# Two transformer blocks on one core: the U products of the expert layer as 512 columns, and one-hot rows by a compare with a pointer

## The chip, the cores and the metric

One Trainium2 chip, one NeuronCore. The metric is the device time of one launch in microseconds (us), as the median over runs.

## The reference

Two blocks run one after the other on 256 tokens of width 1024, all in f32. The first block (attention and a gated feed-forward layer) and the attention and convolution of the second take the first half of the time and are not touched. The change lies in the last layer, a product-key expert layer with 16384 experts. Cut to what matters:

```python
q = (xc @ peer_wq).reshape(TOKEN_CHUNK, PEER_HEADS, PEER_DQ)
v1, i1 = lax.top_k(s1, 16); v2, i2 = lax.top_k(s2, 16)      # s1, s2: scores against 128 keys each
top_s, pos = lax.top_k(v1[..., :, None] + v2[..., None, :], 16)
e = i1 * 128 + i2 at pos;  g = softmax(top_s)                # 8 heads x 16 experts for each token
h = gelu(einsum('cd,chkd->chk', xc, peer_u[e]))
y = einsum('chk,chkd->cd', g * h, peer_v[e])
```

## The kernel before, in words

The kernel does not gather expert rows. It multiplies all 16384 rows of U with all 256 tokens, in 128 blocks of 128 experts, takes the gelu, multiplies it with a gate that is zero for every expert that a token did not choose, and multiplies the result with all rows of V.

**Precision.** TensorE multiplies in fp32r. Each f32 operand is split into a high part (a copy that rounds, on ScalarE) and a low part (the difference, on GpSimd for U, on VectorE for V), and three products are summed: high by high, high weight by low x, low weight by high x.

**U products** (`u_products`, lines 1034 to 1048). For each pair of blocks one PSUM bank `ph` of 512 columns holds two halves of 256 tokens. For each block there are 16 matmuls of 256 columns with the high weights (lines 1042 and 1043: each of the 8 weight chunks is loaded twice, once for `xTh` and once for `xTl`) and 8 with the low weights (line 1046). `u_finish` (line 1050) is called one pair later: it applies the gelu on ScalarE and, for tokens whose gates are there already, multiplies by the gate on VectorE (line 1057).

**Choice of experts** (`choose`, line 909). VectorE finds the top 16 and the indices for each half of the tokens; at the end TensorE transposes the result (`psel`, line 964) and VectorE copies it to `selT` (line 965). The main loop (line 1075) deals out 4000 ns of these steps by fixed estimates to each pair of U blocks, which places 30 blocks ahead of the end of the choice.

**Gates** (`gates`, line 977). For each token a one-hot row of the first key index, times the gate weight in a high and a low part, is multiplied with a one-hot row of the second index: one matmul `pw` of 256 columns (line 1003) gives that token's 128 by 128 gates in two parts. The one-hot rows are made by `choices` (line 985) for four tokens at once: line 990 compares an iota with both indices (1024 elements per partition), line 992 multiplies the first half of that with the two gate parts (1024 elements). ScalarE then copies parts of `pw` out (lines 1009 and 1011), VectorE adds or multiplies them into the tables `GA` and `GB` (lines 1013, 1016, 1019). The function `between` (line 1088) deals the 128 token pairs out over the U blocks that are left but four, in quarters of a block pair.

**V products** (line 1102) come last: 512 columns each, three for each weight part, with the gated activations as stationary operand. They need the gates of all tokens.

**What sets the order.** The program is written in one order; a scheduler turns that into one queue for each engine when the kernel is built, and on the chip each queue runs in order, with waits on semaphores. PSUM has 8 banks: four under tag `a` (the bank of `gate`, and those of `ph`), four under tag `b` (`scratch` with the iota, and `pw`). The raw weights come in by DMA from the SP queue (line 1028), four blocks deep, with three buffers each for the split parts.

Of the kernel before, what the change touches and what calls it, by code (L numbers as in the profile page):

```python
# [10 lines left out]
F32 = mybir.dt.float32  # L11
F32R = mybir.dt.float32r
U32 = mybir.dt.uint32
AF = mybir.ActivationFunctionType
ALU = mybir.AluOpType
# [3 lines left out]
P = 128  # L19
T = 256  # L20
D = 1024
KC = D // P
# [32 lines left out]
def block_pair_kernel(ctx: ExitStack, tc: tile.TileContext, x, gains, convw, norm_final, w_in, w_up_a, w_up_b,  # L55
                      w_out, w_gate, w_up, w_down, w_in_2, qg, kg, w_out_2, wq, keys, u_t, v_tab, final_g,
                      rope1, rope2, masks, out, dbg=None):
    nc = tc.nc
    mm = nc.tensor.matmul
# [6 lines left out]
    def bank(tag, name):  # L66
        return ps.tile([P, 512], F32, tag=tag, name=name)
# [83 lines left out]
    with ExitStack() as dense:  # L151
# [8 lines left out]
        low = {"every": 2}  # L160
# [72 lines left out]
        def xt_pair(pool, tag, kc=KC):  # L233
            return (pool.tile([P, kc, T], F32R, tag=tag + "h", name=tag + "h"),
                    pool.tile([P, kc, T], F32R, tag=tag + "l", name=tag + "l"))
# [287 lines left out]
        with ExitStack() as b2:  # L523
# [15 lines left out]
            for c0 in range(0, DFF, 512):  # L539
# [28 lines left out]
                for i, w_ in enumerate((cwh.bitcast(F32), cwl)):  # L568
                    sh = [P, j1 - j0, P]
# [20 lines left out]
            for b in range(2):  # L590
                drain(gemm_tok(fT, w_down, NFF, 512 * b, 512, add_to_x(b), "fd"))
                feat_split(hT, X, gnf, "n3", range(4 * b, 4 * b + 4))
                sl = slice(512 * b, 512 * b + 512)
# [250 lines left out]
            nc.sync.dma_start(dbg["x3"], X)  # L844

        peer = ctx.enter_context(tc.tile_pool(name="peer", bufs=1, side="right", reuse_waits="tile"))
        xT = xt_pair(peer, "xT")
        selT = peer.tile([P, 3, T], F32, tag="selT", name="selT")
        up = ctx.enter_context(tc.tile_pool(name="up", bufs=2, side="right", reuse_waits="tile"))
        tkx = ExitStack()  # L850
# [4 lines left out]
        iota = scratch[:, 0:P]  # L855
# [114 lines left out]
    def parts(lo, hi):  # L970

        for t_, base, n in ((GA, 0, BLK_A), (GB, BLK_A, NBLK - BLK_A)):
            a, b = max(lo, base), min(hi, base + n)
            if a < b:
                yield t_[:, a - base:b - base], a, b

    def gates(tk2):

        gate = bank("a", "gate").rearrange("p (a t) -> p a t", a=2)
        gh = up.tile([P, 2, T], F32R, tag="gh", name="gsh")[:, 0]  # L980
        nc.scalar.copy(gh, selT[:, 2])
        nc.vector.tensor_copy(gate[:, 0], gh.bitcast(F32))
        nc.vector.tensor_sub(gate[:, 1], selT[:, 2], gh.bitcast(F32))

        def choices(t4):

            sh = [P, 2, 4, P]
            eq = tk2.tile(sh, F32R, tag="eq", name=f"eq_{t4}")
            o1 = tk2.tile(sh, F32R, tag="o1", name=f"o1_{t4}")
            nc.vector.tensor_tensor(eq, iota.unsqueeze(1).unsqueeze(1).to_broadcast(sh),  # L990
                                    selT[:, 0:2, t4:t4 + 4].unsqueeze(3).to_broadcast(sh), op=ALU.is_equal)
            nc.vector.tensor_tensor(o1, eq[:, 0].bitcast(F32).unsqueeze(1).to_broadcast(sh),  # L992
                                    gate[:, :, t4:t4 + 4].unsqueeze(3).to_broadcast(sh), op=ALU.mult)
            return eq, o1

        now = choices(0)
        for t4 in range(0, T, 4):
            ahead = None
            for i in range(2):
                t0 = t4 + 2 * i  # L1000
                pw = bank("b", f"pw{t0}").rearrange("p (j a n) -> p j a n", j=2, a=2)
                for j in range(2):
                    mm(pw[:, j], lhsT=now[0][:, 1, 2 * i + j], rhs=now[1][:, :, 2 * i + j], start=True, stop=True)  # L1003
                if i == 0 and t4 + 4 < T:
                    ahead = choices(t4 + 4)
                x_ = done["blocks"]
                if x_:
                    w_ = up.tile([P, 2, P], F32, tag="gll", name=f"w_{t0}")
                    nc.scalar.copy(w_[:, :, :x_], pw[:, :, 1, :x_])
                for g, a, b in parts(x_, NBLK):  # L1010
                    nc.scalar.copy(g[:, :, t0:t0 + 2].rearrange("p b t -> p t b"), pw[:, :, 1, a:b])
                if x_:
                    nc.vector.tensor_tensor(pw[:, :, 0, :x_], pw[:, :, 0, :x_], w_[:, :, :x_], op=ALU.add)
                for g, a, b in parts(0, x_):
                    g = g[:, :, t0:t0 + 2].rearrange("p b t -> p t b")
                    nc.vector.tensor_tensor(g, pw[:, :, 0, a:b], g, op=ALU.mult)
                for g, a, b in parts(x_, NBLK):
                    g = g[:, :, t0:t0 + 2].rearrange("p b t -> p t b")
                    nc.vector.tensor_tensor(g, pw[:, :, 0, a:b], g, op=ALU.add)
                done["tokens"] = t0 + 2  # L1020
                if i == 0:
                    yield 1
            now = ahead
            yield 1

    def load_block(src, i, name, eng):
        raw = up.tile([P, D], F32, tag="raw", name=f"{name}raw{i}", bufs=4)
        nc.sync.dma_start(raw, src)
        hi = up.tile([P, D], F32R, tag="hi", name=f"{name}hi{i}", bufs=3)
        lo = up.tile([P, D], F32R, tag="lo", name=f"{name}lo{i}", bufs=3)  # L1030
        split(hi, lo, raw, eng)
        return hi, lo

    def u_products(b, between=lambda part: None):
        ph = bank("a", f"ph{b}")
        xh, xl = xT
        for i in range(2):
            hi, lo = load_block(u_t[b + i].rearrange("p k e -> p (k e)"), b + i, "u", nc.gpsimd)
            o = ph[:, i * T:(i + 1) * T]
            for k in range(KC):  # L1040
                sl = slice(k * P, (k + 1) * P)
                mm(o, lhsT=hi[:, sl], rhs=xh[:, k], start=k + i == 0, stop=False)  # L1042
                mm(o, lhsT=hi[:, sl], rhs=xl[:, k], start=False, stop=False)  # L1043
            between(2 * i)
            for k in range(KC):
                mm(o, lhsT=lo[:, k * P:(k + 1) * P], rhs=xh[:, k], start=False, stop=k + i == KC)  # L1046
            between(2 * i + 1)
        return b, ph.rearrange("p (b t) -> p b t", b=2)

    def u_finish(b, ph):  # L1050
        n = done["tokens"]
# [22 lines left out]
    b = 0  # L1074
    while spend(steps, 4000) and b < BLK_A:
        now = u_products(b)
        if pending:
            u_finish(*pending)
        pending = now
        b += 2  # L1080
# [3 lines left out]
    GB = gwb.tile([P, NBLK - BLK_A, T], F32, tag="GB", name="GB")  # L1084
    with tc.tile_pool(name="tk2", bufs=2, side="right", reuse_waits="tile") as tk2:
        steps = gates(tk2)
        first, rounds = b, (NBLK - b) // 2 - 2
        def between(part):
            quarter = 4 * ((b - first) // 2) + part + 1
            drain(steps, max(0, -(-(T // 2) * quarter // (4 * rounds)) - done["tokens"] // 2))  # L1090

        while b < NBLK:
            now = u_products(b, between)
            if pending:
                u_finish(*pending)
            pending = now
            b += 2
# [124 lines left out]
```

## Time and profile before

| | us |
|---|---|
| median of 3 runs | 1328.95 |
| lowest and highest run | 1327.55, 1329.12 |
| the profiled execution, its own time | 1327.62 |
| its span, first to last instruction | 1325.8 |
| mean granted TensorE clock | 0.988 |
| PE, VectorE (DVE), ScalarE (ACT), GpSimd (POOL) busy | 97%, 70%, 53%, 50% |

PE is the matmul engine and PEld its weight loads. Matmuls overlap in a pipeline, and so do VectorE instructions to a smaller degree: the duration of one is longer than the time from its start to the start of the next. Where the cost of many in a row is wanted, the distance between starts is the one to read.

### The profile page before, as it was taken

The numbers are of one execution on the slowest core, as the hardware profiler recorded it, in microseconds if no ns is written. First come the engines' busy times: TensorE is split into PE (matmuls) and PEld (weight loads), VectorE is DVE, ScalarE is ACT, GpSimd is POOL, SyncE is SP. The second block draws the span as 40 slices with busy tenths as digits, with TensorE's granted clock in tenths as the row PEclk, the third lists the DMA queues.
The fourth block names the chain that finished last, engine by engine and source line by source line (L and its number), as shares of the span: only waits on it lengthen the run. The fifth ranks groups of instructions, "written<-read, shape, count | busy, mean of one in ns | idle before, by whom it ended". The sixth has DMA issues, their size and how long they took to land.

```text
span 1325.8 us, 22837 instructions
## 1 busy us (share of the span) xinstructions
PE 1286.9 (97%) x8585; PEld 1179.9 (89%) x8585; DVE 925.2 (70%) x1984; ACT 704.6 (53%) x1263; POOL 669.4 (50%) x322
## 2 busy tenths in 40 slices
PE   7799999999999979999999999999999999999997
PEld 7689989999889859999999999999988888888885
DVE  6775546766327964799599999999955555555555
ACT  5256655444456736454566666656544444444443
POOL 5565485777468728567877777777700000000001
PEclk9899999999999979999999999999999999999999
DMA  8343344654754415245655555555566666666663
GB/s 294 132 159 128 128 159 159 193 189 130 237 173 144 144 64 193 79 131 172 180 169 162 165 169 161 165 169 161 161 197 197 192 191 195 194 195 193 191 192 109
DMA packets 85646, 222.65 MB, mean 168 GB/s; under 512 B 6304, under 2 KB 15904, under 8 KB 85536
## 3 DMA queue, kind: packets, MB, share of 16 engines
q1 hardware_dynamic: 84960, 220.12, 52.9%
q8 instruction: 67, 1.10, 0.3%
q10 hardware_dynamic: 576, 1.08, 0.2%
q14 instruction: 43, 0.35, 0.1%
HBM read 220.13 MB, written 1.05 MB: 167 GB/s over the span
## 4 chain that ended last, share of the span: by engine, by line
PE 89%; DVE 7%; ACT 2%; DMA 1%; issue 0%; POOL 0%; SPq 0%; ACTq 0%; DVEq 0%
PE po L1107 26%; PE ph L1042 8%; PE ph L1043 8%; PE ph L1046 8%; PE pw L1003 2%; PE fu L221 2%; PE fu L220 2%; PE fg L222 2%; PE fu L222 2%; PE fg L221 2%; PE fg L220 2%; PE fd L197 2%; PE fd L199 2%; PE fd L198 2%; PE g L220 1%; PE wq L221 1%
## 5 line engine op out<-in xcount | busy, mean ns | idle before, releaser
L121 POOL TENSOR_TENSOR wlo<-raw,whi 128x1024 fp32r<-128x1024 f32 (+3 forms) x134 | 301.1, 2254 | 184.9 <-ACT whi L120 171.7
L121 POOL TENSOR_TENSOR ulo<-uraw,uhi 128x1024 fp32r<-128x1024 f32 x128 | 309.2, 2418 | 110.6 <-PE ph L1046 47.5
L120 ACT CAST whi<-raw 128x1024 fp32r<-128x1024 f32 (+3 forms) x174 | 167.9, 970 | 192.5 <-PE fd L198 30.5
L121 DVE TENSOR_TENSOR vlo<-vraw,vhi 128x1024 fp32r<-128x1024 f32 x128 | 157.1, 1227 | 153.2 <-ACT vhi L120 153.2
L1042 PE MATMUL ph<-xTh,uhi 128*128 128x256 f32 x1024 | 252.9, 284 | 0.0
L1043 PE MATMUL ph<-xTl,uhi 128*128 128x256 f32 x1024 | 252.5, 284 | 0.0
L120 ACT CAST vhi<-vraw 128x1024 fp32r<-128x1024 f32 x128 | 135.0, 1055 | 180.2 <-PE po L1107 175.4
L120 ACT CAST uhi<-uraw 128x1024 fp32r<-128x1024 f32 x128 | 134.5, 1052 | 157.1 <-issue 109.0
L1042 PEld LDWEIGHTS ph<-xTh,uhi 128*128 128x128 f32 x1024 | 197.6, 193 | 0.2 <-DVE GB L1057 0.2
L1043 PEld LDWEIGHTS ph<-xTl,uhi 128*128 128x128 f32 x1024 | 197.4, 193 | 0.0
L1143 POOL TENSOR_TENSOR X<-X,fg 128x512 f32<-128x512 f32 x4 | 5.1, 1279 | 351.5 <-ACT GA L1140 351.5
L1046 PE MATMUL ph<-xTh,ulo 128*128 128x256 f32 x1024 | 144.0, 283 | 0.0
L1107 PE MATMUL po<-vhi,gh 128*128 128x512 f32 x512 | 138.3, 389 | 0.0
L1107 PE MATMUL po<-vhi,gll 128*128 128x512 f32 x512 | 138.3, 389 | 0.0
L1107 PE MATMUL po<-vlo,gh 128*128 128x512 f32 x512 | 138.3, 389 | 0.0
L1046 PEld LDWEIGHTS ph<-xTh,ulo 128*128 128x128 f32 x1024 | 132.2, 192 | 0.0
L1107 PEld LDWEIGHTS po<-vlo,gh 128*128 128x128 f32 x512 | 96.1, 188 | 20.0
L1107 PEld LDWEIGHTS po<-vhi,gll 128*128 128x128 f32 x512 | 96.1, 188 | 20.0
L1107 PEld LDWEIGHTS po<-vhi,gh 128*128 128x128 f32 x512 | 96.0, 188 | 19.8
L121 DVE TENSOR_TENSOR wlo<-raw,whi 128x1024 fp32r<-128x1024 f32 (+3 forms) x40 | 62.3, 1566 | 48.0 <-ACT whi L120 47.7
L990 DVE TENSOR_TENSOR eq<-scratch,selT 128x1024 fp32r<-128x1024 f32 x64 | 77.9, 1218 | 2.8 <-PE pw L1003 2.6
L992 DVE TENSOR_TENSOR o<-eq,gate 128x1024 fp32r<-128x1024 f32 x64 | 77.5, 1212 | 0.0
(430 smaller groups left out, 2871.7 us busy)
## 6 DMA issues: line engine op xcount, KB each, us to landing
uraw<-in_u_t_dram SPq DMA_DIRECT2D x128, 512.0 KB, 3.6
vraw<-in_v_tab_dram SPq DMA_DIRECT2D x128, 512.0 KB, 4.3
raw<-in_w_in_dram SPq DMA_DIRECT2D x18, 1024.0 KB, 5.0
raw<-in_w_gate_dram SPq DMA_DIRECT2D x10, 1024.0 KB, 5.0
raw<-in_w_up_dram SPq DMA_DIRECT2D x10, 1024.0 KB, 5.1
raw<-in_w_down_dram SPq DMA_DIRECT2D x10, 1024.0 KB, 5.6
raw<-in_wq_dram SPq DMA_DIRECT2D x8, 1024.0 KB, 5.1
raw<-in_w_out_dram SPq DMA_DIRECT2D x6, 1024.0 KB, 5.2
```

Of the source, the lines that this page charges most:

```text
L120: nc.scalar.copy(hi, src)
L121: (eng or nc.vector).tensor_sub(lo, src, hi.bitcast(F32))
L197: mm(o, lhsT=xh[:, k, sl], rhs=wh[:, :cols], start=k == 0 and (c == 0 or 2 * cols > 512), stop=False)
L220: mm(view[n], lhsT=h_[:, sl], rhs=xh[:, k_], start=k_ == 0 and n % 2 == 0, stop=False)
L221: mm(view[n], lhsT=h_[:, sl], rhs=xl[:, k_], start=False, stop=False)
L222: mm(view[n], lhsT=l_[:, sl], rhs=xh[:, k_], start=False, stop=k_ == K - 1 and (n % 2 == 1 or n == nb - 1))
L990: nc.vector.tensor_tensor(eq, iota.unsqueeze(1).unsqueeze(1).to_broadcast(sh), selT[:, 0:2, t4:t4 + 4].unsqueeze(3).to_broadcast(sh), op=A ...
L992: nc.vector.tensor_tensor(o1, eq[:, 0].bitcast(F32).unsqueeze(1).to_broadcast(sh), gate[:, :, t4:t4 + 4].unsqueeze(3).to_broadcast(sh), op ...
L1042: mm(o, lhsT=hi[:, sl], rhs=xh[:, k], start=k + i == 0, stop=False)
L1043: mm(o, lhsT=hi[:, sl], rhs=xl[:, k], start=False, stop=False)
L1046: mm(o, lhsT=lo[:, k * P:(k + 1) * P], rhs=xh[:, k], start=False, stop=k + i == KC)
L1107: mm(po[2 * c + n], lhsT=gt[:, b % 2, c * P:(c + 1) * P], rhs=vt[:, n * 512:(n + 1) * 512], start=b == 0 and step == 0, stop=b == NBLK - 1 ...
```

## The change

The high and the low part of x now lie in one tile `xTb`. For each block a bank `ph` of its own holds 512 columns: the product of a high weight chunk with both parts of x is one matmul of 512 columns (8 for each block in place of 16 of 256), the 8 products of the low weights go into the first half as before. ScalarE copies the second half to SBUF (`plow`), and VectorE adds it to the first half, into the pair's first bank. In the gates the gate parts stay in SBUF (no PSUM bank), only the second index is compared for four tokens at once (512 elements), and the scaled one-hot row of the first index is made by one `scalar_tensor_tensor` for each token (256 elements; the index comes through a pointer to one value per partition).

```diff
--- before.py
+++ after.py
@@ -844,7 +844,8 @@
             nc.sync.dma_start(dbg["x3"], X)
 
         peer = ctx.enter_context(tc.tile_pool(name="peer", bufs=1, side="right", reuse_waits="tile"))
-        xT = xt_pair(peer, "xT")
+        xTb = peer.tile([P, 2, KC, T], F32R, tag="xT", name="xT")
+        xT = xTb[:, 0], xTb[:, 1]
         selT = peer.tile([P, 3, T], F32, tag="selT", name="selT")
         up = ctx.enter_context(tc.tile_pool(name="up", bufs=2, side="right", reuse_waits="tile"))
         tkx = ExitStack()
@@ -976,21 +977,22 @@
 
     def gates(tk2):
 
-        gate = bank("a", "gate").rearrange("p (a t) -> p a t", a=2)
-        gh = up.tile([P, 2, T], F32R, tag="gh", name="gsh")[:, 0]
-        nc.scalar.copy(gh, selT[:, 2])
-        nc.vector.tensor_copy(gate[:, 0], gh.bitcast(F32))
-        nc.vector.tensor_sub(gate[:, 1], selT[:, 2], gh.bitcast(F32))
+        gsh = up.tile([P, 2, T], F32R, tag="gh", name="gsh")
+        gate = gsh.bitcast(F32)
+        nc.scalar.copy(gsh[:, 0], selT[:, 2])
+        nc.vector.tensor_sub(gate[:, 1], selT[:, 2], gate[:, 0])
 
         def choices(t4):
 
-            sh = [P, 2, 4, P]
-            eq = tk2.tile(sh, F32R, tag="eq", name=f"eq_{t4}")
-            o1 = tk2.tile(sh, F32R, tag="o1", name=f"o1_{t4}")
-            nc.vector.tensor_tensor(eq, iota.unsqueeze(1).unsqueeze(1).to_broadcast(sh),
-                                    selT[:, 0:2, t4:t4 + 4].unsqueeze(3).to_broadcast(sh), op=ALU.is_equal)
-            nc.vector.tensor_tensor(o1, eq[:, 0].bitcast(F32).unsqueeze(1).to_broadcast(sh),
-                                    gate[:, :, t4:t4 + 4].unsqueeze(3).to_broadcast(sh), op=ALU.mult)
+            eq = tk2.tile([P, 4, P], F32R, tag="eq", name=f"eq_{t4}")
+            o1 = tk2.tile([P, 4, 2, P], F32R, tag="o1", name=f"o1_{t4}")
+            nc.vector.tensor_tensor(eq, iota.unsqueeze(1).to_broadcast([P, 4, P]),
+                                    selT[:, 1, t4:t4 + 4].unsqueeze(2).to_broadcast([P, 4, P]), op=ALU.is_equal)
+            for j in range(4):
+                t = t4 + j
+                nc.vector.scalar_tensor_tensor(o1[:, j], iota.unsqueeze(1).to_broadcast([P, 2, P]), selT[:, 0, t:t + 1],
+                                               gate[:, :, t].unsqueeze(2).to_broadcast([P, 2, P]),
+                                               op0=ALU.is_equal, op1=ALU.mult)
             return eq, o1
 
         now = choices(0)
@@ -1000,7 +1002,7 @@
                 t0 = t4 + 2 * i
                 pw = bank("b", f"pw{t0}").rearrange("p (j a n) -> p j a n", j=2, a=2)
                 for j in range(2):
-                    mm(pw[:, j], lhsT=now[0][:, 1, 2 * i + j], rhs=now[1][:, :, 2 * i + j], start=True, stop=True)
+                    mm(pw[:, j], lhsT=now[0][:, 2 * i + j], rhs=now[1][:, 2 * i + j], start=True, stop=True)
                 if i == 0 and t4 + 4 < T:
                     ahead = choices(t4 + 4)
                 x_ = done["blocks"]
@@ -1032,20 +1034,19 @@
         return hi, lo
 
     def u_products(b, between=lambda part: None):
-        ph = bank("a", f"ph{b}")
-        xh, xl = xT
-        for i in range(2):
+        phs = [bank("a", f"ph{b}_{i}").rearrange("p (a t) -> p a t", a=2) for i in range(2)]
+        low = up.tile([P, 2, T], F32, tag="plow", name=f"plow{b}")
+        for i, ph in enumerate(phs):
             hi, lo = load_block(u_t[b + i].rearrange("p k e -> p (k e)"), b + i, "u", nc.gpsimd)
-            o = ph[:, i * T:(i + 1) * T]
             for k in range(KC):
-                sl = slice(k * P, (k + 1) * P)
-                mm(o, lhsT=hi[:, sl], rhs=xh[:, k], start=k + i == 0, stop=False)
-                mm(o, lhsT=hi[:, sl], rhs=xl[:, k], start=False, stop=False)
+                mm(ph, lhsT=hi[:, k * P:(k + 1) * P], rhs=xTb[:, :, k], start=k == 0, stop=False)
             between(2 * i)
             for k in range(KC):
-                mm(o, lhsT=lo[:, k * P:(k + 1) * P], rhs=xh[:, k], start=False, stop=k + i == KC)
+                mm(ph[:, 0], lhsT=lo[:, k * P:(k + 1) * P], rhs=xTb[:, 0, k], start=False, stop=k == KC - 1)
             between(2 * i + 1)
-        return b, ph.rearrange("p (b t) -> p b t", b=2)
+            nc.scalar.copy(low[:, i], ph[:, 1])
+            nc.vector.tensor_tensor(phs[0][:, i], ph[:, 0], low[:, i], op=ALU.add)
+        return b, phs[0]
 
     def u_finish(b, ph):
         n = done["tokens"]
```

## Rows read from the trace of the kernel before

**Rows 1.** the page, busy time, and the 40 slices of DVE

```profile
PE 1286.9 (97%) x8585; PEld 1179.9 (89%) x8585; DVE 925.2 (70%) x1984; ACT 704.6 (53%) x1263; POOL 669.4 (50%) x322
...
DVE  6775546766327964799599999999955555555555
```

**Rows 2.** the page, the chain that ended last

```profile
PE po L1107 26%; PE ph L1042 8%; PE ph L1043 8%; PE ph L1046 8%; PE pw L1003 2%; PE fu L221 2%; PE fu L220 2%; PE fg L222 2%; PE fu L222 2%; PE fg L221 2%; PE fg L220 2%; PE fd L197 2%; PE fd L199 2%; PE fd L198 2%; PE g L220 1%; PE wq L221
```

**Rows 3.** windows: us; PE, PEld, DVE, ACT, POOL busy; clock, DMA share, GB/s

```profile
563.60:655.40 91.80, 89.01 (x732) 88.80 (x732) 77.03 (x232) 46.71 (x54) 69.59 (x30) 0.98 0.54 161
655.40:959.10 303.70, 303.70 (x2529) 303.36 (x2528) 291.86 (x688) 185.50 (x497) 228.76 (x95) 1.00 0.54 165
959.10:968.70 9.60, 9.60 (x82) 9.60 (x81) 5.60 (x7) 4.89 (x7) 3.66 (x2) 1.00 0.56 184
```

**Rows 4.** timeline of PE, one block of U: start us, us, instruction

```profile
601.18 0.28 PE L1042 MATMUL ph<-xTh,uhi 128*128 128x256 f32 x1
...
603.10 1.12 PE L1046 MATMUL ph<-xTh,ulo 128*128 128x256 f32 x8
604.06 0.27 PE L964 MATMUL psel<-ident,sel 128*128 128x128 f32 x1
```

**Rows 5.** timeline of PE, products of 512 columns in the V stage

```profile
1101.01 1.07 PE L1107 MATMUL po<-vlo,gh 128*128 128x512 f32 x4
...
1101.91 1.07 PE L1107 MATMUL po<-vhi,gh 128*128 128x512 f32 x4
```

**Rows 6.** timeline of VectorE, one round of one-hot tiles

```profile
843.80 1.21 DVE L990 TENSOR_TENSOR eq<-scratch,selT 128x1024 fp32r<-128x1024 f32 x1
844.93 0.34 DVE L1013 TENSOR_TENSOR pw<-pw,w 128x172 f32<-128x172 f32 x1
845.17 1.21 DVE L992 TENSOR_TENSOR o<-eq,gate 128x1024 fp32r<-128x1024 f32 x1
846.30 0.45 DVE L1016 TENSOR_TENSOR GA<-pw,GA 128x128 f32<-128x128 f32 x1
```

**Rows 7.** timeline of VectorE, five scalar_tensor_tensor with a pointer

```profile
535.75 2.05 DVE L136 SCALAR_TENSOR_TENSOR xTl<-pt_n,gn,xTh 128x256 fp32r<-128x256 f32 x5 [1.60 <-ACT xTh L134]
```

**Rows 8.** timeline of VectorE, instructions of 256 elements back to back

```profile
457.16 0.48 DVE L703 SCALAR_TENSOR_TENSOR cacc<-hc,cw,cacc 128x256 f32<-128x256 f32 x1
457.55 0.42 DVE L339 TENSOR_TENSOR mixl<-pv_C,mixh 128x256 fp32r<-128x256 f32 x1
457.88 0.48 DVE L703 SCALAR_TENSOR_TENSOR cacc<-hc,cw,cacc 128x256 f32<-128x256 f32 x1
```

**Rows 9.** timeline of VectorE, end of the gates, and two tensor_tensor of 512

```profile
958.68 0.17 DVE L1019 TENSOR_TENSOR GB<-pw,GB 128x16 f32<-128x16 f32 x1
958.88 1.29 DVE L1057 TENSOR_TENSOR GB<-ph,GB 128x512 f32<-128x512 f32 x2
960.09 1.28 DVE L121 TENSOR_TENSOR gll<-GA,gh 128x512 fp32r<-128x512 f32 x2
```

**Rows 10.** groups of VectorE from 655.4 to 959.1: busy, mean ns, idle before

```profile
L990 DVE TENSOR_TENSOR eq<-scratch,selT 128x1024 fp32r<-128x1024 f32 x64 | 77.9, 1218 | 2.8 <-PE pw L1003 2.6
L992 DVE TENSOR_TENSOR o<-eq,gate 128x1024 fp32r<-128x1024 f32 x64 | 77.5, 1212 | 0.0
...
L1013 DVE TENSOR_TENSOR pw<-pw,w 128x56 f32<-128x56 f32 (+42 forms) x128 | 39.7, 314 | 7.8 <-ACT GB L1011 7.2
```

**Rows 11.** timeline of VectorE, start of the gates

```profile
655.36 0.56 DVE L965 COPY selT<-psel 128x384 f32<-128x384 f32 x1 [13.13 <-PE psel L964]
```

**Rows 12.** waits of PE in the choice of experts: total us, times, longest

```profile
PE psel L964 <- DVE sel L955: 2.8, 1, 2.8
```

**Rows 13.** timeline of PE, last gate product and first product of V

```profile
955.88 0.40 PE L1003 MATMUL pw<-o,eq 128*128 128x256 f32 x2
...
968.61 0.63 PE L1107 MATMUL po<-vhi,gh 128*128 128x512 f32 x2
```

**Rows 14.** groups of ScalarE by shape, copies of 256 elements from PSUM

```profile
L321 ACT COPY pT_B<-ptp_B 128x256 f32<-128x256 f32 x4 | 1.4, 385 | 0.0
```

## The prediction

> **What bounds the kernel now.** I read the page first. PE is busy 97% of the span [rows 1] and the chain that ended last runs on PE almost throughout [rows 2], so fewer matmul columns or closer matmuls should help. But in the 40 slices, of 33.1 us each, VectorE (DVE) stands at nine tenths as well in the nine slices from 663 to 961 us [rows 1]. That is the stage of the change, so the next view is a table by stage [rows 3]. It cuts the stage in three: the choice of experts (563.6 to 655.4, 30 blocks of U), the gates (655.4 to 959.1, the other 98 blocks less the last ones) and a tail until V begins at 968.7. In the gates PE has no gap at all, and VectorE is busy 291.9 of 303.7 us: it has 11.8 us, 4%, to spare, where ScalarE (ACT) has 118 and GpSimd (POOL) 75. Two engines are near their limit together. A change that takes work from one and gives work to the other is decided by which of them has it more.
>
> **PE's part.** The distance between starts is read off the timelines. A block's 16 products with high weights run from 601.18 to 603.10, 0.120 us each, and its 8 with low weights to 604.06, also 0.120 [rows 4]. Products of 512 columns, each with a weight load of its own, stand 0.225 us apart (four in 0.90) [rows 5]. A block goes from 16 x 0.120 = 1.92 to 8 x 0.225 = 1.80: 0.12 us, and 15 us over 128 blocks. The saving is small because the columns stay the same; only the distance beyond them shrinks.
>
> The Trainium skill, page "TensorE: Matmul & The Clock Gate", section "Back-to-back issue gap", gives columns over 2.4 GHz plus 2.5 ns for one matmul behind another: 109 ns for 256 columns, so that halving the count would save 8 x 2.5 ns a block, 2.6 us in all. The rows disagree at 256 columns (120 ns); by the page the faster rival below would come out near 1325 us, and the forecast, in which PE does not set the end, would stay.
>
> **VectorE's part, per four tokens.** Before: two instructions of 1024 elements, 843.80 to 844.93 and 845.17 to 846.30, 1.13 us each, 2.26 together [rows 6]. After: one compare of 512, and four scalar_tensor_tensor of 256 with a pointer. Two of 512 take 1.21 us from the start of the first to the start of what follows (958.88 to 960.09), 0.605 each [rows 9]. Five scalar_tensor_tensor of 256 with the same kinds of operand (PSUM, pointer and SBUF in, fp32r out) last 2.05 us together [rows 7]; less the last one's 0.48 that is 0.39 from start to start, as it is at 457.16 [rows 8]. So 0.605 + 4 x 0.39 = 2.165 us: a quarter fewer elements buy only 0.095 us, because each small instruction pays again for its start. Over 64 rounds [rows 10]: -6.1 us. The copy of the gate's high part that falls away is worth 0.3. Bounds: 0.33 is what a tensor_tensor of 256 without a pointer takes [rows 8], and then the rounds save 21.5 us; 0.48 is the whole duration, if nothing overlaps, and then they cost 17 us more than before. I take 0.39, from the row with the same operands.
>
> **VectorE's part, per block.** One tensor_tensor of 256 elements is new (PSUM and SBUF in, PSUM out): 0.33 us from start to start, the tensor_tensor of 256 at 457.55 [rows 8]. Bound above: its duration, 0.42; below there is no reason for less than 0.33. For 30 blocks ahead of the gates that is 9.9 us, for the other 98 it is 32.3 us (41 at the bound).
>
> The Trainium skill, page "VectorE: DVE Perf Modes", section "The TRN2 errata — SBUF-src ops pay a fixed extra latency per instruction", counts 120 cycles plus one per element for an instruction that reads PSUM, 0.392 us at 256 elements. The pointer instruction agrees (0.39), the plain one does not (0.33); by the page the adds would cost 6 us more.
>
> **ScalarE's part.** One copy of 256 elements out of PSUM for each block, 0.385 us [rows 14], 38 us in the gates, beside 118 idle. It costs nothing itself; GpSimd, the DMAs on SP's queue and the splits of U stay as they are. Uncovered it is the second rival.
>
> **What waits for what.** The add waits for ScalarE's copy, the copy for the block's last product. Behind the add in VectorE's queue stand the next one-hot rows and the work on `pw`; behind those waits PE, which can't run a `pw` product without `eq` and `o1`, nor start a block before a bank under `a` is free (four, two for each pair, now that `gate` holds none).
>
> **The sum.** The profiled execution took 1327.6 us for a span of 1325.8; the median of the runs is 1.3 above it.
> - *Start of the gates: -2.8 us.* VectorE was done with the choice 13.13 us before `selT` came at 655.36, that is at 642.2; it waited for the transposes in PE's queue [rows 11]. With 9.9 us of adds it is done at 652.1; PE, 30 x 0.12 earlier, is there at 651.2. Bound: 0, as PE already waited 2.8 us for VectorE at the transposes of the first half [rows 12], and will wait longer.
> - *VectorE's work in the gates: 32.3 - 6.1 - 0.3 = +25.9 us.* PE's work there shrinks by 98 x 0.12 = 11.8, so VectorE sets the pace.
> - *Its idle time: -5.9 us.* Of the 11.8 us, 7.2 were waits for ScalarE and 2.6 for PE [rows 10]. With VectorE as the bound part of these go; I take half, between none and all.
> - *Tail: -4.5 us.* From VectorE's last gate to V lie 9.6 us [rows 3], the products of the last four blocks that follow the last `pw` at 955.88 [rows 13]. If PE keeps its order they remain (-0.5); if it has run ahead, only some 1.5 us of splitting remain (-8.1). I take the middle.
>
> Together +12.7 us: **1340 us**, 0.9% slower. What is late next is V's first product, which needs the gates of all tokens; V itself is untouched. With these bounds the forecast's own range is 1331 (everything hidden that can be: -2.8 + 25.9 - 11.8 - 8.1 = +3.2) to 1353 (nothing: +25.4).
>
> **The rivals.**
> - *Faster: the pointer compare is cheap.* At 0.33 us for each the rounds save 21.5 us and VectorE's work grows by 32.3 - 21.5 - 0.3 = 10.5 us, less than its 11.8 us of idle time. PE stays the bound and gives its 15 us: 1313 us. It turns at about 0.34 us an instruction. For it: instructions of 256 elements without a pointer do reach 0.33 [rows 8]. Against: none with a pointer does, in rows 7 and 8. Chance 0.13.
> - *Slower still: the add waits at the head of the queue.* A copy `plow` that stands behind a split of U on ScalarE (1.05 us) holds the add, and VectorE, which has nothing to spare, stands. If that hits one block in four, 98 / 4 x 1.05 = 26 us come on top: 1366 us. For it: the same pattern, VectorE behind ScalarE's copies of `pw`, cost 7.2 us in 16 waits of up to 1.2 us [rows 10]. Against: an idle ScalarE for 39% of the stage [rows 3]. Chance 0.12.
> - *No change: all slack is used.* The forecast at its low end, VectorE without a gap and PE far enough ahead, with about 1 us less for the smaller terms: 1326 to 1331 us. Chance 0.10.
> - *Slower as worked out,* 1331 to 1353 and somewhat beyond: 0.65.
>
> **The numbers.** A measurement of this kernel can tell 0.2%, 2.7 us, from no change. Faster 0.13, same 0.10, slower 0.65 + 0.12 = 0.77. The range 1324 to 1358 holds the forecast, with a few us for adds at 0.42 in place of 0.33, and the case of no change; the rivals at 1313 and 1366 are left out.
>
> **What would show it.** In the profile after: 512-column products in `ph` 0.225 us apart; the pointer instructions 0.39 us apart; VectorE without idle time from the copy of `selT` to the last gate, over a stretch of some 320 us in place of 304; PE with gaps before `pw` or `ph` that VectorE ends; V beginning near 981. The forecast is wrong if PE still has no gap in the gates (then the pointer instruction or the add is cheaper than its row), and its size is wrong if VectorE idles there for ScalarE.

## The result: 1342.2 us, 1.1% slower, as forecast in sign and size

The changed kernel takes 1342.16 us (median of 4 runs, 1341.93 to 1344.21) against 1328.49 us before, where a fourth run now counts. The ratio is 1.0107, with a 95% interval of 1.0089 to 1.0124: 13.7 us more.

The profiled execution takes 1344.21 us for a span of 1342.4; it is the longest of the four, the spans of the others are 1340.2 to 1340.4. Its U products begin at 565.9 us in place of 563.6. That part of the program is unchanged, and in the profiles of the experiments below the same start lies anywhere between 564.0 and 566.3, so it is not counted as part of the change. From the first U product to the first V product it takes 419.2 us, before 404.9: 14.3 us more, which is the change in this execution. About 1.3 us of that belong to a stretch of half TensorE clock inside the gates, which the last section shows.

The windows by stage of the kernel after, in the columns of [rows 3]: choice of experts, gates, tail, V.

```profile
565.90:655.50 89.60, 86.94 (x491) 75.90 (x490) 85.47 (x261) 55.28 (x83) 69.57 (x30) 0.98 0.53 164
655.50:974.00 318.50, 302.17 (x1761) 264.80 (x1760) 311.50 (x972) 209.77 (x588) 225.85 (x94) 0.99 0.50 156
974.00:985.10 11.10, 11.10 (x66) 9.76 (x65) 9.91 (x12) 7.20 (x13) 4.81 (x2) 1.00 0.61 179
985.10:1342.40 357.30, 348.43 (x1538) 288.14 (x1537) 201.18 (x226) 169.45 (x200) 5.11 (x4) 0.99 0.59 186
```

The gates last 318.5 us in place of 303.7, and now it is VectorE that has almost no gap: 311.5 us busy, before 291.9. PE has fewer instructions (1761, before 2529) and stands still for 16.3 us. The chain that ended last, which the profile follows back to 664 us, now holds VectorE with 12% of the span; before it ran on PE almost throughout [rows 2]:

```profile
PE 35%; DVE 12%; issue 2%; ACT 1%; ACTq 0%; DVEq 0%
PE po L1108 26%; PE ph L1042 6%; DVE o L993 4%; PE ph L1045 3%; DVE GA L1018 2%; DVE pw L1015 1%; DVE GB L1021 1%; DVE eq L989 1%; DVE ph L1048 1%; DVE GB L1018 1%; PE pw L1005 1%; DVE GB L1058 0%; ACT uhi L120 0%; ACT GB L1013 0%; ACT w L1
```

The parts of the change, in the timeline of VectorE: an add (L1048), the compare (L989) and four pointer instructions in one merged row (L993).

```profile
846.47 0.46 DVE L1048 TENSOR_TENSOR ph<-ph,plow 128x256 f32<-128x256 f32 x1
846.80 0.71 DVE L989 TENSOR_TENSOR eq<-scratch,selT 128x512 fp32r<-128x512 f32 x1
847.40 1.68 DVE L993 SCALAR_TENSOR_TENSOR o<-scratch,selT,gsh 128x256 fp32r<-128x256 f32 x4
848.96 0.36 DVE L1015 TENSOR_TENSOR pw<-pw,w 128x168 f32<-128x168 f32 x1
```

From start to start: the add 0.33 us, the compare 0.60, the four pointer instructions 1.56, that is 0.39 each. All three stand as priced; where a round of one-hot rows took 2.26 us [rows 6] it takes 2.16.

PE's side, one block of U in the timeline: 8 products of 512 columns with a wait ahead of them, 8 of 256, two `pw`, and the next block.

```profile
700.05 2.09 PE L1042 MATMUL ph<-xT,uhi 128*128 128x512 f32 x8 [0.74 <-DVE ph L1048]
701.98 1.11 PE L1045 MATMUL ph<-xT,ulo 128*128 128x256 f32 x8
702.93 0.40 PE L1005 MATMUL pw<-o,eq 128*128 128x256 f32 x2
703.16 2.00 PE L1042 MATMUL ph<-xT,uhi 128*128 128x512 f32 x8
705.01 1.12 PE L1045 MATMUL ph<-xT,ulo 128*128 128x256 f32 x8
```

The 8 products from 703.16 to 705.01 stand 0.231 us apart, not 0.225 as in V [rows 5]. The wait of 0.74 us at 700.05 is for an add: PE needs a bank that VectorE has not yet emptied. The waits in the gates, in total us, times, longest:

```profile
PE ph L1042 <- DVE ph L1048: 12.3, 14, 1.1
...
PEld ph L1042 <- ACT GB L1013: 10.2, 11, 1.3
DVE pw L1015 <- ACT GB L1013: 6.7, 10, 1.7
...
PE ph L1042 <- ACT GB L1013: 2.2, 4, 0.8
DVE selT L966 <- PE psel L965: 1.8, 1, 1.8
PE pw L1005 <- DVE o L993: 1.3, 3, 0.5
...
DVE ph L1048 <- ACT plow L1047: 0.2, 1, 0.2
```

PE waits, where before it had no gap: 12.3 us for VectorE's add and 2.2 us for ScalarE's copies. The row of PEld is no further loss: its waits are mostly the same pauses, seen by the weight load ahead of the waiting product. VectorE waits 6.7 us for ScalarE, about as before [rows 10].

### The profile page after: what moved, and what is told of

Same layout as the page of the kernel before. It is cut to its first block, busy times and chain, and to the rows that moved or that the text cites. A ratio compares the mean times of both kernels' runs of the same rounds, so it can differ in the third digit from the quotient of the medians.

```text
span 1342.4 us, 21334 instructions
## 1 busy us (share of the span) xinstructions
PE 1286.4 (96%) x7561; PEld 1129.5 (84%) x7561; DVE 958.1 (71%) x2303; ACT 740.0 (55%) x1391; POOL 668.0 (50%) x322
## 3 DMA queue, kind: packets, MB, share of 16 engines
q10 hardware_dynamic: 576, 1.08, 0.2%
## 4 chain that ended last, share of the span: by engine, by line
PE 35%; DVE 12%; issue 2%; ACT 1%; ACTq 0%; DVEq 0%
PE po L1108 26%; PE ph L1042 6%; DVE o L993 4%; PE ph L1045 3%; DVE GA L1018 2%; DVE pw L1015 1%; DVE GB L1021 1%; DVE eq L989 1%; DVE ph L1048 1%; DVE GB L1018 1%; PE pw L1005 1%; DVE GB L1058 0%; ACT uhi L120 0%; ACT GB L1013 0%; ACT w L1011 0%
## 5 line engine op out<-in xcount | busy, mean ns | idle before, releaser
L1042 PE MATMUL ph<-xT,uhi 128*128 128x512 f32 x1024 | 262.2, 398 | 17.7 <-DVE ph L1048 15.0
L1042 PEld LDWEIGHTS ph<-xT,uhi 128*128 128x128 f32 x1024 | 185.3, 190 | 55.3 <-ACT GB L1013 10.2
L1045 PEld LDWEIGHTS ph<-xT,ulo 128*128 128x128 f32 x1024 | 138.2, 191 | 7.6
L1045 PE MATMUL ph<-xT,ulo 128*128 128x256 f32 x1024 | 143.7, 283 | 0.0
L993 DVE SCALAR_TENSOR_TENSOR o<-scratch,selT,gsh 128x256 fp32r<-128x256 f32 x256 | 106.4, 487 | 0.0
L1048 DVE TENSOR_TENSOR ph<-ph,plow 128x256 f32<-128x256 f32 x128 | 55.9, 437 | 1.3 <-ACT plow L1047 1.3
L1018 DVE TENSOR_TENSOR GA<-pw,GA 128x128 f32<-128x128 f32 (+17 forms) x128 | 53.4, 417 | 0.0
L1005 PE MATMUL pw<-o,eq 128*128 128x256 f32 x256 | 51.4, 286 | 1.3 <-DVE o L993 1.3
```

Of the source, the lines that this page charges most:

```text
L993: nc.vector.scalar_tensor_tensor(o1[:, j], iota.unsqueeze(1).to_broadcast([P, 2, P]), selT[:, 0, t:t + 1], gate[:, :, t].unsqueeze(2).to_b ...
L1005: mm(pw[:, j], lhsT=now[0][:, 2 * i + j], rhs=now[1][:, 2 * i + j], start=True, stop=True)
L1042: mm(ph, lhsT=hi[:, k * P:(k + 1) * P], rhs=xTb[:, :, k], start=k == 0, stop=False)
L1045: mm(ph[:, 0], lhsT=lo[:, k * P:(k + 1) * P], rhs=xTb[:, 0, k], start=False, stop=k == KC - 1)
L1048: nc.vector.tensor_tensor(phs[0][:, i], ph[:, 0], low[:, i], op=ALU.add)
```

## The experiments

The theory was that VectorE's total of work in the gates decides the time. The rivals were that the pointer instructions or the latency of the new links (product, copy, add, bank) do, whatever the total. Medians stand against 1328.99 to 1329.11 us for the kernel before on the same chip.

**The one-hot rows alone.** Edit against the changed kernel: `u_products` as before.

```diff
-        phs = [bank("a", f"ph{b}_{i}").rearrange("p (a t) -> p a t", a=2) for i in range(2)]
...
+        ph = bank("a", f"ph{b}")
...
+                mm(o, lhsT=hi[:, sl], rhs=xh[:, k], start=k + i == 0, stop=False)
+                mm(o, lhsT=hi[:, sl], rhs=xl[:, k], start=False, stop=False)
...
```

> The rows by the pointer compare alone; the U products as before (256 columns, one bank for a pair, no add). Theory (VectorE's throughput decides): 64 rounds at 2.165 in place of 2.26 us take 6.1 us from VectorE, PE sets the pace as before: 1326 to 1330 us, PE without a gap in the gates, VectorE idle there 16 to 20 us in place of 11.8. Rival (the pointer instructions themselves hold the one-hot rows up, four short links in place of one long one): 1333 us or more, PE waiting for the rows.

Measured: 1328.66 us, ratio 0.9997 (0.9987 to 1.0006). The gates in its windows:

```profile
655.90:959.80 303.90, 303.11 (x2526) 302.91 (x2525) 287.37 (x878) 185.57 (x495) 227.97 (x95) 1.00 0.55 165
```

The stage is as long as before; VectorE is busy 287.4 us in place of 291.9, so 16.5 us of it are free. The pointer rows save a little work on an engine that was not the bound, and cost nothing.

**The add taken away.** This kernel leaves the product with the low part of x out of the sum.

```diff
-            nc.scalar.copy(low[:, i], ph[:, 1])
-            nc.vector.tensor_tensor(phs[0][:, i], ph[:, 0], low[:, i], op=ALU.add)
+            if i == 0:
+                nc.scalar.copy(low[:, i], ph[:, 1])
+            else:
+                nc.scalar.copy(phs[0][:, i], ph[:, 0])
```

> The changed kernel without the add on VectorE: for the second block ScalarE copies the first half straight into the pair's first bank, and the product with the low part of x is left out of the sum. The banks, the number of ScalarE's copies and PE's products stay. Theory (VectorE's throughput): its work in the gates falls by 31 us, below PE's; PE is the bound and gives its 15 us against the kernel before: 1312 to 1316 us. Rival (two banks for a pair, with ScalarE's copy between, hold PE up by themselves): 1325 us or more, with PE waiting for ScalarE or banks. A middle value gives the share of each.

Measured: 1324.38 us, ratio 0.9963 (0.9950 to 0.9976). Without the adds 17.8 of the changed kernel's 1342.2 us are gone, the whole loss and some gain. But the gain against the kernel before is 4.6 us, not 15, and the value lies at the edge of the rival's. Its gates and waits there:

```profile
654.50:955.20 300.70, 296.43 (x1764) 262.56 (x1763) 285.75 (x877) 215.02 (x590) 227.74 (x95) 1.00 0.52 166
```

```profile
PEld ph L1042 <- ACT ph L1050: 5.1, 8, 0.8
...
PE ph L1042 <- ACT ph L1050: 3.4, 8, 0.6
```

VectorE is busy 285.8 of 300.7 us. Two things keep PE's gain small: the saving is less than was priced (at 0.231 us a block saves 1.92 - 1.85 = 0.07 us, 9 us in all), and PE now waits at eight places for ScalarE's copy out of the bank that it needs. The two rows show the same eight pauses, 3.4 us by PE and 5.1 by its weight loads, and are not to be added. So the rival mechanism exists, with a share of some us; the adds carry the loss. This run alone does not tell VectorE's work from the add's place between two banks, as it takes both away; the next one does.

**A dose of VectorE work.** The rows of the first index by a compare and a product without a pointer; the results are the same.

```diff
...
-            for j in range(4):
-                t = t4 + j
-                nc.vector.scalar_tensor_tensor(o1[:, j], iota.unsqueeze(1).to_broadcast([P, 2, P]), selT[:, 0, t:t + 1],
-                                               gate[:, :, t].unsqueeze(2).to_broadcast([P, 2, P]),
-                                               op0=ALU.is_equal, op1=ALU.mult)
+            for o, a in ((eq, 1), (o1[:, 1], 0)):
+                nc.vector.tensor_tensor(o, iota.unsqueeze(1).to_broadcast([P, 4, P]),
+                                        selT[:, a, t4:t4 + 4].unsqueeze(2).to_broadcast([P, 4, P]), op=ALU.is_equal)
+            sh = [P, 2, 4, P]
+            nc.vector.tensor_tensor(o1, o1[:, 1].bitcast(F32).unsqueeze(1).to_broadcast(sh),
+                                    gate[:, :, t4:t4 + 4].unsqueeze(3).to_broadcast(sh), op=ALU.mult)
...
```

> The changed kernel with the rows of the first index made by two plain tensor_tensor (a compare of 512 elements, a product of 1024) in place of four pointer instructions; the results are the same. On VectorE a round is 0.60 + 0.60 + 1.13 = 2.33 us in place of 2.165, 10.6 us more over 64 rounds; PE, ScalarE and the banks see no difference. Theory (throughput): 1351 to 1354 us, the whole 10.6 us. Rival (the loss comes from the latency of copy, add and bank, not from VectorE's total): 1341 to 1345 us.

Measured: 1399.61 us, ratio 1.0530 (1.0512 to 1.0548): 57.4 us above the changed kernel, and outside both expectations. The dose was larger than meant. The group of the products and the window of the gates:

```profile
L993 DVE TENSOR_TENSOR o<-o,gsh 128x1024 fp32r<-128x1024 f32 x64 | 124.1, 1940 | 0.0
```

```profile
655.40:1030.90 375.50, 323.41 (x1764) 279.44 (x1764) 367.95 (x843) 212.74 (x590) 243.67 (x95) 0.94 0.41 133
```

The product of 1024 elements takes 1940 ns, where the same shape took 1212 before [rows 10]. VectorE's busy time in the gates rose by 367.95 - 311.50 = 56.5 us, the stage by 57.0, the kernel by 57.4. The run missed its number for the size of the dose, and shows the theory better for it: each us by which VectorE is longer occupied in the gates is a us of the kernel. Why the product is slow is told at the end.

**The tail.** The gates are dealt out over one more pair of blocks.

```diff
-        first, rounds = b, (NBLK - b) // 2 - 2
+        first, rounds = b, (NBLK - b) // 2 - 1
```

> The changed kernel with the gates dealt out over one more pair of U blocks (48 in place of 47), so that two blocks in place of four follow the last gate product. VectorE's and PE's work is the same. Theory (the products that follow the gates are not hidden, as PE keeps its order; VectorE sets the pace before them): the tail of 11.0 us shrinks by the 5.5 us of two blocks: 1336 to 1339 us. Rival (PE catches up in any case, or VectorE's last splits hold V's start): 1341 to 1344 us.

Measured: 1334.23 us, ratio to before 1.0044 (1.0027 to 1.0060): 7.9 us less than the changed kernel, and 1.8 us below the expected range. Gates and tail:

```profile
655.10:969.20 314.10, 304.64 (x1793) 268.02 (x1792) 312.73 (x973) 211.55 (x592) 230.91 (x96) 1.00 0.52 162
969.20:974.80 5.60, 5.60 (x35) 4.93 (x34) 5.37 (x10) 4.21 (x8) 0.00 (x0) 1.00 0.66 191
```

The tail falls from 11.1 to 5.6 us, as expected for two blocks. The rest comes from the gates, 4.4 us shorter with 1.2 us more of VectorE work: its idle time there goes from 7.0 to 1.4 us. Some 1.3 us of these belong to the stretch of half clock, which this execution does not have in its gates. PE keeps its order, and what stands behind the last gate product is paid in full while VectorE is the bound.

**Where the 512-column products stand 0.231 us apart.**

```diff
-        xTb = peer.tile([P, 2, KC, T], F32R, tag="xT", name="xT")
-        xT = xTb[:, 0], xTb[:, 1]
+        xTb = peer.tile([P, KC, 2, T], F32R, tag="xT", name="xT")
+        xT = xTb[:, :, 0], xTb[:, :, 1]
...
-                mm(ph, lhsT=hi[:, k * P:(k + 1) * P], rhs=xTb[:, :, k], start=k == 0, stop=False)
+                mm(ph, lhsT=hi[:, k * P:(k + 1) * P], rhs=xTb[:, k], start=k == 0, stop=False)
...
```

> The changed kernel with the two parts of x side by side for each chunk, so that the moving operand of a 512-column product is one run of 512 elements in place of two of 256 that lie 2048 elements apart. It is to tell why these products stand 0.231 us apart in U and 0.226 in V. If the two runs cost it: 0.226 here, the time unchanged within 0.3% (VectorE is the bound). If it is something else (the accumulation into one bank, the weights' layout): 0.231 as before.

Measured, in one run: 1343.19 us. One block in the timeline of PE:

```profile
601.89 2.00 PE L1042 MATMUL ph<-xT,uhi 128*128 128x512 f32 x8
603.73 1.12 PE L1045 MATMUL ph<-xT,ulo 128*128 128x256 f32 x8
```

1.84 us for 8, 0.230 each: the two runs of 256 elements are not the cause. Over all blocks of the changed kernel the last three of the eight stand 0.227 us apart, as all products of V do (medians); the excess is in the first five, 0.228 to 0.236. Why stays open.

**512 columns where VectorE has room.** If the total decides, the wide products should pay in the choice of experts, in the tail, and for some of the blocks beside the gates. The edit chooses by pair (here every fourth; `u_narrow` is the kernel before's `u_products`).

```diff
+    def u_products(b, between=None):
+        kw = {} if between is None else {"between": between}
+        p = (b - first) // 2 if between else 0
+        return (u_wide if between is None or p >= rounds or p % 4 == 3 else u_narrow)(b, **kw)
```

> 512-column products with the add only where VectorE has room by the profile: the 30 blocks ahead of the gates and the last 4; the 94 blocks beside the gates have 256-column products as before. The pointer rows are kept. Theory (VectorE's throughput): PE saves 34 x 0.12 = 4.1 us and VectorE's work in the gates is 6 us below that of before, so PE's saving shows: 1323 to 1326 us. Rival (the add's latency holds PE up in the choice of experts, as two gaps of 2.0 and 1.2 us there in the changed kernel suggest): 1327 to 1331 us.

> As mix0, with one pair of blocks in four beside the gates (11 of 47 pairs) in 512 columns too. VectorE in the gates: 291.9 - 6.4 + 22 x 0.33 = 292.8 us of work, PE 303.7 - 22 x 0.12 = 301.1 us. Theory (throughput): PE still the bound, 2.6 us less than mix0: 1320 to 1324 us. Rival (each add in the queue costs PE a wait): 1326 us or more.

> As mix0, with every second pair of blocks beside the gates (23 of 47) in 512 columns. VectorE in the gates: 291.9 - 6.4 + 46 x 0.33 = 300.7 us, PE 303.7 - 46 x 0.12 = 298.2 us: the two cross here, and with some idle time of VectorE the result stands above mix4. Theory (throughput): 1323 to 1330 us, some half of the way between mix0 and the changed kernel or less. Rival (PE's saving rules up to here): 1318 us.

> mix2 (every second pair beside the gates in 512 columns) with the gates dealt out over one more pair of blocks. In mix2 VectorE had 7.4 us idle and PE 9.5 us of gaps: both near their limit. Theory: the longer stretch takes load off VectorE and one pair less follows the gates; 2 to 5 us less than mix2's 1327: 1322 to 1325 us. Rival (the tail is PE's own work, whose place does not matter while PE is the bound): 1326 to 1328 us.

> As mix2_tail with every third pair beside the gates in 512 columns. PE has 2.4 us more of work than there, VectorE some 5 us less. Theory (PE the bound again): PE's work 394 us and 6 us of gaps, 4.9 us less than before: 1323 to 1326 us. Rival (as mix2_tail or above): 1326 to 1328 us.

| kernel | wide pairs beside the gates | median, us | ratio to before (95%) |
|---|---|---|---|
| mix0 | none | 1327.05 | 0.9984 (0.9975 to 0.9993) |
| mix4 | one in four | 1326.04 | 0.9975 (0.9964 to 0.9985) |
| mix2 | one in two | 1326.99 | 0.9981 (0.9972 to 0.9990) |
| mix2_tail | one in two, tail of one pair | 1325.86 | 0.9977 (0.9968 to 0.9986) |
| mix3_tail | one in three, tail of one pair | 1325.20 | 0.9977 (0.9967 to 0.9986) |
| the change | all | 1342.16 | 1.0107 (1.0089 to 1.0124) |

All five are below the kernel before, by 2 to 4 us, but not as far as expected: mix0 fits its rival, mix4 stands 2 us above its range, mix2 in it, mix2_tail above it, mix3_tail in it. The time of mix4 would fit its rival too, but the rival's waits are not there: PE waits 0.4 us in its gates. The five intervals overlap, so no order among the kernels rests on them. Two causes show for the missing gain: a block saves 0.07 us and not 0.12, and in the choice of experts PE still waits for the add. In the timeline of PE in mix0:

```profile
577.39 2.11 PE L1058 MATMUL ph<-xT,uhi 128*128 128x512 f32 x8 [1.75 <-DVE ph L1064]
...
585.72 1.69 PE L1058 MATMUL ph<-xT,uhi 128*128 128x512 f32 x6 [2.48 <-DVE ph L1064]
```

There the add stands in VectorE's queue behind the choice: at the first wait behind one instruction of 2.2 us, at the second behind a string of short ones that keeps adds away for 7.3 us. Still the series says what the theory says: beside the gates the wide products are free as long as VectorE has room, and from none to half of the pairs the time does not rise; with all of them it is 15 us higher.

## Why the prediction was right

**What bounds the kernel: right.** VectorE's 96% in the gates was the number that decided. The dose and the kernel without adds show it: 56.5 us more of VectorE's time made 57.4 us, and taking the adds away gave 17.8 us back.

**PE's part: mis-sized, without effect on the forecast.** The price of 0.225 us for a product of 512 columns was read in V; in U it is 0.231. (Over all of V the median is 0.227; a row of four is read 0.002 too low.) A block saves 0.07 us, not 0.12, and all blocks 9 us, not 15. By the formula for an isolated gap of the Trainium skill, page "TensorE: Matmul & The Clock Gate", section "Back-to-back issue gap", it would have been 2.6 us; the trace stands between the two. The error matters where PE is the bound: the mixed kernels gained less than expected.

**VectorE's part: right in each price.** A pointer instruction was priced at 0.39 and measured at 0.39, the compare at 0.605 and 0.60, the add at 0.33 and 0.33. So a quarter fewer elements did buy only 0.1 us a round, and the faster rival, which needed 0.34 for a pointer instruction, fell. Its 1313 us was also wrong by the prediction's own numbers. With 10.5 us more, VectorE would have had 302.4 us of work in the gates, and PE after its saving only 291.9: VectorE would have set the pace, and nearly all of PE's 11.8 us there would have been lost.

**ScalarE's part: nearly right.** The copies themselves were covered. But PE waited 2.2 us in the gates for ScalarE's copies, and 3.4 us for them in the kernel without adds: there the copy is a link between a product and the bank for a later one, and has a price once VectorE is no longer the bound.

**The sum, term by term,** in the profiled execution:

| term | forecast | measured | from |
|---|---|---|---|
| start of the gates | -2.8 | -2.2 | 89.6 in place of 91.8 |
| VectorE's work in the gates | +25.9 | +19.6 | 311.5 in place of 291.9 |
| its idle time | -5.9 | -4.8 | 7.0 in place of 11.8 |
| tail | -4.5 | +1.5 | 11.1 in place of 9.6 |
| together | +12.7 | +14.1 | |

Two terms missed by 6 us each, in opposite directions, and cancelled. The sign and the bound were foreseen; that the number came within 2.2 us of the measured one is luck.

*The start of the gates* came near its value in another way. PE set it, not VectorE, which still waited 1.8 us for the transposes: 30 blocks at 0.07 us are 2.1 us. (PE's own 651.2 in the prediction should read 651.8, which is 655.36 less 30 x 0.12.)

*The tail* failed: the middle was taken between a PE that keeps its order and one that has run ahead. PE kept its order; five blocks follow the last `pw`, with a wait for ScalarE ahead of them. The timeline of PE there, which answers to [rows 13]:

```profile
969.74 0.64 PE L1005 MATMUL pw<-o,eq 128*128 128x256 f32 x4
971.14 2.06 PE L1042 MATMUL ph<-xT,uhi 128*128 128x512 f32 x8 [0.76 <-ACT GB L1013]
...
984.21 1.11 PE L1045 MATMUL ph<-xT,ulo 128*128 128x256 f32 x8
985.16 0.63 PE L1108 MATMUL po<-vhi,gh 128*128 128x512 f32 x2
```

The run with one pair less there confirms that it is paid: 5.5 us.

*VectorE's work* grew by 6 us less than the sum of its parts. From start to start over the whole stage, the adds came to +31.2 us (four of the 98 fell into the tail), the rounds to -6.9, the making of the gate parts to +0.4 in place of -0.3: 24.7 together. The other 5 us went out of instructions that the change does not touch, above all those on `pw`: L1013 took 31.5 us from start to start, and the same instructions as L1015 take 28.7. An instruction that the next one overlaps costs its distance, one that nothing follows costs its whole duration, some 0.08 us more (1.21 against 1.13 in [rows 6]). Of VectorE's instructions in the gates, 68 had ended before the next began; in the changed kernel, whose VectorE is always behind, 15. By these numbers that is an estimated 53 x 0.08 = 4.2 us, most of the 5. So the busier VectorE overlapped more, and its old work got cheaper.

**Slower still** fell too: in the gates VectorE waited for `plow` once, for 0.2 us. In a queue that is always behind, the copy was done long before the add's turn came. **No change** needed a PE that has run ahead, and fell with the tail.

## What to carry to other kernels

When two engines are both near their limit in a stage, price a change by what it adds to the second, instruction by instruction, from start to start; the gain on the first comes only as far as the second has room. A few large instructions split into many small ones keep their fixed cost each, so count the instructions before the elements. And work that follows the last result of the engine that sets the pace is paid in full as long as its own queue keeps its order: deal the slow engine's work out to the very end.

## What the runs showed of the hardware that was not expected

**VectorE with both operands in SBUF waits for GpSimd.** The product of 1024 elements in the dose took 1940 ns on average. Before, with the gate parts in PSUM, it took 1212, and in the changed kernel the pointer instructions, which read the iota from PSUM, are not slowed. Of the 64 products in the dose, 38 began while GpSimd split a block of U, and each of them ended 1.08 to 1.09 us after the split. The other 26 took 1.20 to 1.22 us; during 16 of these a split began, and it ended 2.2 us or more after the product, where a split alone takes 2.4 us. One that began during a split, in the timeline of VectorE and then of GpSimd:

```profile
846.42 2.72 DVE L993 TENSOR_TENSOR o<-o,gsh 128x1024 fp32r<-128x1024 f32 x1
```

```profile
845.72 2.34 POOL L121 TENSOR_TENSOR ulo<-uraw,uhi 128x1024 fp32r<-128x1024 f32 x1 [0.42 <-PE pw L1004]
```

GpSimd ends at 848.06, VectorE at 849.14, 1.08 us later: about the time that the product takes alone. The Trainium skill, page "SBUF — State Buffer", section "SBUF: two separate sides", calls the port pair that the two engines share an exclusive lock that whoever starts first holds for its whole instruction; this trace agrees, in all 54 cases. The changed kernel has one such instruction, the gate's low part, which took 1.18 us in place of 0.42. It read two SBUF operands before as well, but began 0.02 us ahead of a split there; here a split ran from 655.35 to 657.76.

```profile
656.86 1.18 DVE L983 TENSOR_TENSOR gsh<-selT,gsh 128x256 f32<-128x256 f32 x1
```

**The same gap can halve PE's clock, or not.** In the changed kernel a wait of 1.11 us for an add in the gates is followed by 8 products that take 3.62 us in place of 2.0; the granted clock there is 0.50, the lower of the two levels, 1.2 GHz. The run with the parts of x side by side has the same wait at the same place, and its products take 2.08 us, at 1.00. PE's row and the window in the changed kernel:

```profile
920.64 3.62 PE L1042 MATMUL ph<-xT,uhi 128*128 128x512 f32 x8 [1.11 <-DVE ph L1048]
```

```profile
920.80:924.10 3.30, 3.30 (x9) 2.53 (x9) 3.30 (x12) 0.54 (x2) 0.05 (x1) 0.50 0.54 161
```

The same in the run with the parts side by side:

```profile
921.08 2.08 PE L1042 MATMUL ph<-xT,uhi 128*128 128x512 f32 x8 [1.11 <-DVE ph L1048]
```

```profile
921.10:924.10 3.00, 3.00 (x17) 2.65 (x18) 3.00 (x11) 1.54 (x4) 0.20 (x1) 1.00 0.54 193
```

The gates last 318.5 us in the one and 317.2 in the other, so by this pair the half clock cost about 1.3 us. In the choice of experts it cost nothing. There, after a wait of 1.74 us, 8 products took 3.49 us at a granted clock of 0.55, and the next wait for an add was 0.91 us, where the run with the parts side by side waited 2.47:

```profile
579.08 3.49 PE L1042 MATMUL ph<-xT,uhi 128*128 128x512 f32 x8 [1.74 <-DVE ph L1048]
```

```profile
579.10:582.40 3.30, 3.30 (x9) 2.59 (x10) 3.30 (x16) 0.60 (x1) 0.86 (x1) 0.55 0.67 220
```
